# A hybrid decoder trunk on one core: block order, a delayed sum and an earlier last norm in the second layer's down stage

## The chip, the cores and the metric

The kernel runs on one core of a Trainium2 chip. The metric is device time in microseconds (us), from the start to the end of one execution; a kernel's time is the median of its runs. The core has five engines with a queue of instructions each: TensorE (PE, matmuls, with its weight loads listed as PEld), VectorE (DVE), ScalarE (ACT), GpSimd (POOL), and SyncE (SP), which here only issues transfers. Each queue is worked off in order: an instruction that waits holds up everything behind it on its engine. Transfers run beside the engines.

## The reference

Two layers, each a token mixer and a feed-forward part (SwiGLU), each with an RMSNorm that is shifted and scaled by a conditioning vector in front, and a gated residual sum behind. The sequence has 1024 tokens of 1024 channels, the feed-forward part 2816 hidden channels. The stack ends with one more RMSNorm. Cut to what matters here:

```
def swiglu_ffn(h, w_gate, w_up, w_down):
    return (jax.nn.silu(h @ w_gate) * (h @ w_up)) @ w_down

for i in range(DEPTH):                      # DEPTH = 2
    ...
    y = swiglu_ffn(h, ffn_w_gate[i], ffn_w_up[i], ffn_w_down[i])
    x = x + (1.0 + g_f)[:, None, :] * y
return rms_norm(x, final_g)
```

All in float32. The change is in how the last `@ w_down` (i = 1), the last sum into x, and the last `rms_norm` are ordered.

## The kernel before

**Layout.** x is held with channels on the 128 partitions: eight tiles of 128 channels for each of two chunks of 512 tokens, chunk A (first) and chunk B. A float32 operand is split into a high part (a cast on ScalarE) and a low part (the difference, on VectorE); a product is then three matmuls: high by high, high by low, low by high (`products`). Every matmul goes through line 148, every recorded operation of VectorE, ScalarE and GpSimd through line 126 and the transfers of SP through lines 158 and 1449; so the profile's lines say little, and the tile names tell the operations apart: `dn` is a bank of the down product, `w` a weight's parts, `raw` and `s` weights as loaded or summed, `op` an operand as loaded, `hi` and `lo` its parts, `t` and `acc` squares and their sums, `var` the mean of squares and `rstd` the reciprocal root spread over the partitions, `ny` its copy.

**Seven products.** The second layer's down product is done with seven block products (Strassen's way) instead of eight. The weight is split in four blocks by even and odd hidden tiles and by the two halves of the output channels, the operand by even and odd hidden tiles and by the two chunks. Class `Seven` runs a list of steps: each block product (p2, p1, p5, p6, p7, p4, p3) is a loop over groups q = 0 to 5 of hidden tiles. Eleven pairs of tiles make five full groups of two (24 matmuls) and one short one, q = 5, with one (12 matmuls). p2's groups 0 to 3 are done earlier (`one_half`); p3's groups in `LAST` = (2, 3, 4) are left to `ending`.

Two sets of four PSUM banks, x and y, collect the products. p2 uses y; p1 starts x; p5 starts y; p6, p7 and p4 go on adding to what is in x; p3 starts y. With the last group of each block product, as soon as a bank has its last matmul, `update` on VectorE adds gate times the bank to the x tile of a chunk and half:

```
last = q == qs[-1] and j == len(ops) - 1
products(bs[d], wt, 4 * j + d, g, fresh and q == qs[0] and j == 0, last, more=True)
if last:
    for ch, half in ends:
        update(ch, 4 * half + d, bs[d], gate_f, self.l)
```

Within a group the banks are worked in two pairs, (0, 1) and then (2, 3), each over the group's one or two operand tiles. The next block product on the same banks cannot write a bank before its update has read it.

**Weights and operands of a group.** `weights_of` loads the weight block on SP; for `s1` (p5) and `s4` (p3) a second load on POOL's queue adds another block to it in flight, and can start only when the first has landed. A block of sums (`st["sum", q]`, tile `s`) is held over the stage: p1 loads a11 into it, p5 takes its own sum off it, p6 uses it as its weight, p7 adds it to its load, p3 adds a12 to it and uses it. `halves` makes the parts of the weight; in p5 it also issues the subtraction from the held block, right behind the weight's low part and ahead of the operand's parts. `operand` loads the operand (written to memory by the joint stage before: the last store, for group 5, is made at the end of that stage). `Seven.load` runs LOADED = 4 groups ahead, `Seven.split` SPLIT = 2 groups ahead. Chunk B's x comes back from memory in four transfers, m = 0 to 3, one behind each of p1's groups q = 0 to 3 (`x_in`, the dictionary given to `seven.run`).

**What sets the order.** TensorE's order is the order of the code. On the other engines a scheduler places the instructions by a simulated timeline and by priority; `tc.add_manual_dep(later, earlier, edge)` fixes the order of two. Background work is written as generators (`Task`) that `pace` steps between groups of matmuls, by model clocks of the engines. A generator may yield a name; the task then rests until the model clock of TensorE has passed the later of VectorE's and ScalarE's clocks by a delay from these tables (the second for a task in the background, as here):

```
DELAY = {"stats": 2.75, "spread": 3.0, "soon": 0.5, "settled": 3.0, "later": 5.0, "root": 3.4}
DELAY_BEHIND = {"stats": 8, "spread": 4, "soon": 0.5, "settled": 3.0, "later": 8}
```

**The last norm.** `final(A)` is such a task. It squares and sums chunk A's tiles (the second half once p4 is through), then calls `mean_rsqrt`: rest by `when`, matmuls for the mean, eight short VectorE instructions for the reciprocal root, rest, matmuls that spread the root, a copy. Then it multiplies the eight tiles, five on GpSimd, three on VectorE, and stores them. Chunk B's last norm is in `ending`: p3's last groups and B's first output half, in two halves of 256 tokens, four banks each, with the updates, squares and sums on the way, and a norm for each half.

Of the kernel before, what the change touches and what calls it, by code (L numbers as in the profile page):

```python
# [14 lines left out]
MUL, ADD, SUB = ALU.mult, ALU.add, ALU.subtract  # L15
# [45 lines left out]
NQ = -(-NP // 2)  # L61
LAST = (2, 3, 4)
# [69 lines left out]
def trunk(ctx, tc, xT, c, vec, ada, adan, w1f, w1, wdg, w2, wgu, wdn, wds, wpl, out):  # L132
# [3 lines left out]
    V_ = Engine(nc.vector, "V", clock, PRICES["V"], lambda i: order(i))  # L136
# [391 lines left out]
        V_.scalar_tensor_tensor(y, t, 1.5 * 0.375, y, op0=ADD, op1=MUL)  # L528
        yield

    def mean_rsqrt(acc, n, keep=False, when="stats", loose=False, early=False):

        count = n // P
        parts = acc if isinstance(acc, list) else [acc]
        yield when
        b = bank("var")
        for i in range(count):  # L540
            for a in parts:
                matmul(b[:, i : i + 1], a[:, i * P : (i + 1) * P], ones[:, 0:1], start=a is parts[0], stop=a is parts[-1])
        v, t = b[:, :count], b[:, 16 : 16 + count]
        cols = tmp.tile([P, 16], F32, tag="col1", name=nm("col"), bufs=1)
        col, q = cols[:, :count], cols[:, 8 : 8 + count]
        for _ in rsqrt(v, col, t, q, "T" not in st or "taps_done" in st):
            if loose:
                yield
        V_.spent += 0.2
        clock["V"] += 0.2  # L550
        done = V_.last.ins.name
        for ins in [] if loose else recent + (beside if early else []) + [lows[id(wt)][0] for wt in st.get("loaded", [])[1:] if id(wt) in lows]:
            tc.add_manual_dep(ins, done, edge, reason="behind the root")
        recent.clear()
        yield "spread" if loose else "root"
        r = spare_bank("rstd") if "taps_done" in st else bank("rstd")
        for i in range(count):
            matmul(r[:, i * P : (i + 1) * P], col[:, i : i + 1].broadcast_to([P, P]), ident, start=True, stop=True)
        r = r[:, :n]
        if not keep:  # L560
            return r
        held = temp(n, "ny", 2)
        S_.copy(held, r)
        return held
# [94 lines left out]
    def unit(emit, *weights):  # L659
        units.append((weights, emit))  # L660
# [765 lines left out]
    def weights_of(l, kind, q, placed=True):  # L1426

        n = duo_width(q) * 512
        src = lambda b: wds[q, b][:, :n]
        got = {}  # L1430

        def behind_products(d):
            if placed and last_mm[0] is not None:
                tc.add_manual_dep(d.ins, last_mm[0], edge, reason="behind the products")

        def plus(r, what):
            behind_products(nc.gpsimd.dma_start(r, what, accum_op=ADD))
            clock["G"] = max(clock["G"], clock["PE"]) + 0.9

        def load():  # L1440
            if kind == "a11":
                st["sum", q] = block("h1", "s", F32).rearrange("p a b -> p (a b)")[:, :n]
            if kind in ("a11", "s2", "s4"):
                r = st["sum", q]
            else:
                r = (raw_tile() if placed else raws.tile([P, D], F32, tag="raw", name=nm("raw")))[:, :n]
            first = {"a11": 0, "a12": 1, "a22": 3, "s1": 2, "s3": 3}.get(kind)
            if first is not None:
                behind_products(nc.sync.dma_start(r, src(first)))
            if kind in ("s1", "s4"):  # L1450
                plus(r, src(3 if kind == "s1" else 1))
            got["raw"] = r

        def halves():
            r = got["raw"]
            if kind == "s3":
                V_.tensor_tensor(r, r, st["sum", q], op=ADD)
            wt = wts.tile([P, 2, D], F32R, tag="w", name=nm("w"))
            S_.copy(wt[:, 0, :n], r)
            V_.tensor_tensor(wt[:, 1, :n], r, wt[:, 0, :n].bitcast(F32), op=SUB)  # L1460
            if kind == "s1":
                V_.tensor_tensor(st["sum", q], st["sum", q], r, op=SUB)
            return wt

        return load, halves
# [23 lines left out]
    class Seven:  # L1489
# [13 lines left out]
        def split(self, upto):  # L1503
            while self.splits < min(upto, len(self.parts)):
                self.ready[self.splits] = [part[1]() for part in self.parts[self.splits]]
                self.splits += 1

        def begin(self):
# [132 lines left out]
    def final(ch):  # L1641
        acc = temp(ch.n, "acc", 2)
        for k in range(KT):
# [6 lines left out]
            elif k:  # L1650
                V_.tensor_tensor(acc, acc, sq, op=ADD)
            yield
        steps = mean_rsqrt(acc, ch.n, True, loose=True)
        yield next(steps)
        for k in range(KT):
            S_.activation(x[ch.i][k], x[ch.i][k], AF.Copy, scale=V("final_g", k))
# [273 lines left out]
    def pool_end(ch):  # L1930
# [14 lines left out]
    heads(1, HEADS[1], lambda: None)  # L1945
    unit(lambda take: calm.__setitem__(0, True))
    pool_end(B)
    every = list(range(NQ))
    short = [q for q in every if q not in LAST]
    seven = Seven(1, [  # L1950
        ("p2", "a12", "b21", "y", True, [(A, 0)], [4, 5]),
        ("p1", "a11", "b11", "x", True, [(A, 0)], every),
        ("p5", "s1", "t1", "y", True, [(B, 1), (B, 0)], every),
        ("p6", "s2", "t2", "x", False, [(B, 0)], every),
# [8 lines left out]
    def final_begins():  # L1963
# [2 lines left out]

    seven.run({
        **{("p1", m): lambda m=m: unit(lambda take: x_in(B, m)) for m in range(KT // 2)},
        ("p7", NQ - 1): final_begins,
        ("p4", NQ - 1): lambda: unit(lambda take: st.__setitem__("a_done", True)),  # L1970
    }, last_part)
    run_units(W_BUFS, early)

# [60 lines left out]
```

## Time and profile before

| what | value |
|---|---|
| median of 3 runs | 1707.15 us (1706.41 to 1709.43) |
| the profiled execution | 1708.65 us |
| its span, first to last instruction | 1706.9 us |
| TensorE busy | 1671.0 us, 98% of the span |
| VectorE, ScalarE, GpSimd busy | 77%, 47%, 28% |
| granted TensorE clock, mean | 0.996 of full speed |
| seven products | from about 1492.6 us of the span |
| end of the last product | about 1689.1 us |

The profile is one execution. A row of the timeline gives the start (us from the span's start), the length, the engine, the line, the operation with out<-in and shapes, the count of merged instructions, and in brackets how long the engine was idle before and what ended that. The row of a tile gives the shortest, median and longest length in ns. A row of stretches gives start:end, the length, busy time and count for each engine, then the granted clock, the mean busy share of the 16 transfer engines, and GB/s. A row of the chain gives start, length and what the end of the kernel waited for. Matmuls overlap, so a row of several matmuls is longer than their spacing.

### The profile page before, as it was taken

Reading aid. Unit: us, or ns where it says so; the run is one execution under the profiler, and the core shown is the slowest. Engines: PE = TensorE matmul, PEld = TensorE weight load, DVE = VectorE, ACT = ScalarE, POOL = GpSimd, SP = SyncE. Lnnn points to the kernel's source line nnn. Section 1 sums busy time; section 2 is a strip of 40 time slices with the busy share of each in tenths; the row PEclk is TensorE's granted clock in tenths of the full one; section 3 lists DMA queues with packets and bytes.
Section 4 is the critical chain, followed back from the end, with each engine's and each line's share of the span. In section 5 each row is a group of like instructions: output and inputs, shape, how many; then the busy total and the mean of one; then the engine's idle time right before and its main releaser. Section 6 shows DMA issues by size and latency. Waiting matters only on the chain.

```text
span 1706.9 us, 21328 instructions
## 1 busy us (share of the span) xinstructions
PE 1671.0 (98%) x7614; PEld 1361.9 (80%) x7614; DVE 1318.9 (77%) x1872; ACT 799.5 (47%) x1085; POOL 483.1 (28%) x566
## 2 busy tenths in 40 slices
PE   7999999999999999999999999999999999999996
PEld 5777777778887888888888888888888888887776
DVE  8889899899659887878665987858777767657575
ACT  3669686866546333333213446637222222334353
POOL 3587767796001111211110311101111111010103
PEclk9999999999999999999999999999999999999998
DMA  8858987827776788986877757866777777486822
GB/s 303 286 168 228 237 229 196 220 96 225 225 238 152 253 272 279 294 249 229 342 256 264 250 173 206 241 237 190 189 209 234 217 229 217 169 294 191 241 93 99
DMA packets 115821, 380.71 MB, mean 223 GB/s; under 512 B 12225, under 2 KB 14401, under 8 KB 115714
## 3 DMA queue, kind: packets, MB, share of 16 engines
q1 hardware_dynamic: 77888, 247.46, 41.0%
q0 software_dynamic: 36736, 130.83, 31.2%
q8 instruction: 60, 0.98, 0.2%
q10 hardware_dynamic: 1090, 1.05, 0.2%
q14 instruction: 47, 0.39, 0.1%
HBM read 311.92 MB, written 63.18 MB: 220 GB/s over the span
## 4 chain that ended last, share of the span: by engine, by line
PE 86%; DVE 6%; DMA 3%; ACT 1%; issue 1%; POOL 1%; SPq 0%; DVEq 0%; ACTq 0%
PE a L148 23%; PE dn L148 21%; PE e L148 13%; PE p L148 12%; PE y L148 6%; PE g L148 3%; PE first L148 3%; PE tap L148 2%; DMA raw<-in_wds_dram 2%; POOL pa L126 1%; PE ada L148 1%; DVE t L126 1%; DMA adaw<-in_adan_dram 1%; DMA op<-kinds 1%; DVE x L126 1%
## 5 line engine op out<-in xcount | busy, mean ns | idle before, releaser
L126 ACT CAST w<-raw 128x1024 fp32r<-128x1024 f32 (+1 forms) x249 | 258.9, 1041 | 365.2 <-PE dn L148 99.7
L148 PE MATMUL dn<-g,w 128*128 128x512 f32 x1152 | 265.2, 391 | 1.7 <-DVE g L126 1.0
L126 DVE TENSOR_TENSOR w<-raw,w 128x1024 fp32r<-128x1024 f32 x177 | 217.7, 1233 | 51.2 <-ACT w L126 50.9
L148 PEld LDWEIGHTS dn<-g,w 128*128 128x128 f32 x1152 | 215.7, 188 | 47.6 <-DVE g L126 1.3
L148 PE MATMUL a<-n,w 128*128 128x512 f32 x1056 | 247.7, 390 | 1.1 <-DVE n L126 0.7
L148 PE MATMUL p<-h,w 128*128 128x512 f32 x1056 | 244.2, 391 | 0.9 <-DVE h L126 0.7
L126 POOL TENSOR_TENSOR pa<-pa,pr 128x512 f32<-128x512 f32 x160 | 228.4, 1512 | 23.0 <-ACT pr L126 16.6
L148 PEld LDWEIGHTS a<-n,w 128*128 128x128 f32 x1056 | 197.9, 188 | 44.0 <-DVE n L126 2.2
L148 PEld LDWEIGHTS p<-h,w 128*128 128x128 f32 x1056 | 197.3, 188 | 43.8 <-DVE h L126 1.5
L148 PE MATMUL dn<-hi,w 128*128 128x512 f32 (+1 forms) x600 | 174.3, 373 | 4.3 <-DVE x L126 2.4
L126 DVE SCALAR_TENSOR_TENSOR ca<-u,vecs,ca 128x512 f32<-128x512 f32 x245 | 169.7, 745 | 0.5
L126 DVE SCALAR_TENSOR_TENSOR x<-dn,gains,x 128x512 f32<-128x512 f32 (+1 forms) x144 | 100.9, 730 | 44.7 <-PE dn L148 44.6
L148 PEld LDWEIGHTS dn<-hi,w 128*128 128x128 f32 x600 | 109.8, 188 | 25.6 <-DVE x L126 3.2
L148 PE MATMUL a<-t,w 128*128 128x512 f32 x528 | 123.6, 390 | 0.7 <-DVE w L126 0.7
L148 PE MATMUL e<-b,w 128*128 128x512 f32 x528 | 123.4, 390 | 0.6 <-DVE r L126 0.6
L148 PE MATMUL e<-t,w 128*128 128x512 f32 x528 | 123.3, 389 | 0.0
L126 ACT ACTIVATE pr<-u,vecs 128x512 f32<-128x512 f32 x160 | 108.2, 716 | 26.0 <-POOL pa L126 18.2
L148 PEld LDWEIGHTS a<-t,w 128*128 128x128 f32 x528 | 99.0, 188 | 21.6 <-DVE w L126 1.1
L148 PEld LDWEIGHTS e<-b,w 128*128 128x128 f32 x528 | 99.1, 188 | 21.5 <-DVE r L126 1.0
L1108 POOL DMA_DIRECT2D raw<-in_wgu_dram x41 | 36.2, 884 | 282.5 <-DVE r L126 78.3
L148 PEld LDWEIGHTS e<-t,w 128*128 128x128 f32 x528 | 99.1, 188 | 20.5
L148 PE MATMUL dn<-lo,w 128*128 128x512 f32 (+1 forms) x300 | 111.7, 372 | 0.0
(181 smaller groups left out, 2380.2 us busy)
## 6 DMA issues: line engine op xcount, KB each, us to landing
raw<-in_wgu_dram SPq DMA_DIRECT2D x132, 512.0 KB, 4.8
adaw<-in_ada_dram POOLq DMA_DIRECT2D x48, 512.0 KB, 7.3
raw<-in_wdn_dram SPq DMA_DIRECT2D x44, 512.0 KB, 8.1
raw<-in_wgu_dram POOLq DMA_DIRECT2D x41, 512.0 KB, 7.4
raw<-in_w_dram SPq DMA_DIRECT2D x36, 512.0 KB, 6.2
gd<-g POOLq DMA_DIRECT2D x36, 512.0 KB, 8.1
g<-gd SPq DMA_DIRECT2D x36, 512.0 KB, 6.0
kinds<-k POOLq DMA_DIRECT2D x33, 512.0 KB, 7.3
```

The costliest lines, as they stand in the source:

```text
L126: self.last = self.order(getattr(self.eng, name)(out, *args, **kw))
L148: last_mm[0] = nc.tensor.matmul(out, lhsT, rhs, start=start, stop=stop, skip_group_check=more).ins.name
L1108: d = order(nc.gpsimd.dma_start(w[i], wgu[l, fp, src], accum_op=ADD))
```

## The change

Three things. First, the groups' order in the block products: p1, p5, p6, p7 and p4 run 0, 1, 2, 5, 3, 4 in place of 0 to 5, p2 runs 5, 4 in place of 4, 5, and p3's part in `Seven` runs 0, 5, 1 in place of 0, 1, 5. So each block product ends with a full group; the hooks that hung on the last group of p7 and p4 follow it. The four returns of x stay with groups 0 to 3 of p1. Second, in p5 the subtraction from the held block is issued after the operand's parts, and an order edge puts it behind the operand's low part on VectorE. Third, in `final` the rest ahead of the mean's matmuls becomes "settled" (3.0 in place of 8 for "stats"), and the rest ahead of the spread becomes "soon" (0.5 in place of 4 for "spread").

```
-    def mean_rsqrt(acc, n, keep=False, when="stats", loose=False, early=False):
+    def mean_rsqrt(acc, n, keep=False, when="stats", loose=False, early=False, then=None):
...
-        yield "spread" if loose else "root"
+        yield then or ("spread" if loose else "root")
...
             if kind == "s1":
-                V_.tensor_tensor(st["sum", q], st["sum", q], r, op=SUB)
+                st["then_sum"] = lambda: V_.tensor_tensor(st["sum", q], st["sum", q], r, op=SUB)
...
                 self.ready[self.splits] = [part[1]() for part in self.parts[self.splits]]
+                low = V_.last.ins.name
+                if "then_sum" in st:
+                    tc.add_manual_dep(st.pop("then_sum")().ins, low, edge, reason="behind the low parts")
                 self.splits += 1
...
-        steps = mean_rsqrt(acc, ch.n, True, loose=True)
+        steps = mean_rsqrt(acc, ch.n, True, "settled", loose=True, then="soon")
...
-    every = list(range(NQ))
-    short = [q for q in every if q not in LAST]
+    every = [0, 1, 2, 5, 3, 4]
+    short = [0, 5, 1]
     seven = Seven(1, [
-        ("p2", "a12", "b21", "y", True, [(A, 0)], [4, 5]),
+        ("p2", "a12", "b21", "y", True, [(A, 0)], [5, 4]),
         ("p1", "a11", "b11", "x", True, [(A, 0)], every),
         ("p5", "s1", "t1", "y", True, [(B, 1), (B, 0)], every),
         ("p6", "s2", "t2", "x", False, [(B, 0)], every),
         ("p7", "s3", "t3", "x", False, [(B, 1)], every),
         ("p4", "a22", "t4", "x", False, [(A, 1)], every),
         ("p3", "s4", "b22", "y", True, [(B, 0)], short),
...
-        ("p7", NQ - 1): final_begins,
-        ("p4", NQ - 1): lambda: unit(lambda take: st.__setitem__("a_done", True)),
+        ("p7", every[-1]): final_begins,
+        ("p4", every[-1]): lambda: unit(lambda take: st.__setitem__("a_done", True)),
```

## The prediction

> **What bounds the kernel now.** I read the page first, then the stretches of the second layer's down stage, then TensorE's own timeline there, and last the queues that its waits point to.
>
> ```profile
> PE 1671.0 (98%) x7614; PEld 1361.9 (80%) x7614; DVE 1318.9 (77%) x1872; ACT 799.5 (47%) x1085; POOL 483.1 (28%) x566
> ```
>
> TensorE is busy for 98% of the span, so only its idle stretches and the tail can give time. The stretches (times from the span's start; busy time and count for each engine; then granted clock, DMA share, GB/s):
>
> ```profile
> core 0: us, PE busy (x) PEld busy (x) DVE busy (x) ACT busy (x) POOL busy (x), PEclk, DMA share, GB/s
> 1492.60:1543.64 51.04, 49.56 (x219) 40.74 (x217) 30.02 (x34) 15.67 (x18) 5.97 (x8) 1.00 0.92 292
> 1594.76:1626.49 31.73, 30.46 (x132) 24.63 (x132) 17.62 (x20) 12.86 (x17) 3.54 (x4) 1.00 0.83 237
> 1669.40:1689.10 19.70, 19.68 (x166) 19.44 (x164) 11.20 (x30) 9.78 (x21) 1.46 (x1) 1.00 0.00 1
> 1689.10:1706.90 17.80, 4.77 (x20) 4.42 (x20) 7.89 (x24) 1.67 (x4) 11.68 (x13) 0.59 0.66 236
> 1506.84:1530.71 23.87, 23.87 (x107) 19.75 (x106) 7.24 (x7) 4.57 (x6) 1.79 (x3) 1.00 0.94 308
> ```
>
> The stage starts near 1492.6, its last products end near 1689.1, and 17.8 us of tail follow in which TensorE works 4.8 us. The transfers are nearly full before 1543 and empty from 1669 to 1689. TensorE's timeline (start, length, instruction, idle before it and what ended that) shows all its idle time:
>
> ```profile
> 1543.64 0.74 PE L148 MATMUL dn<-hi,w 128*128 128x512 f32 x2 [1.48 <-DVE w L126]
> ...
> 1594.76 0.50 PE L148 MATMUL dn<-hi,w 128*128 128x512 f32 x1 [1.59 <-DVE x L126]
> ...
> 1624.79 0.47 PE L148 MATMUL dn<-hi,w 128*128 128x512 f32 x1 [0.50 <-ACT w L126]
> ...
> 1626.49 0.50 PE L148 MATMUL dn<-hi,w 128*128 128x512 f32 x1 [0.77 <-DVE x L126]
> ...
> 1692.70 1.23 PE L148 MATMUL rstd<-ident,col 128*128 128x128 f32 x4 [3.62 <-DVE col L126]
> ```
>
> That is 4.34 us of idle in the products, and 3.62 us in front of the ending's first reciprocal root. Together 7.96 us: the most that the change can take from TensorE's waits.
>
> **The unit of time.** From the chain of waits:
>
> ```profile
> 1492.75 24.27 PE dn L148 x107
> ```
>
> 0.227 us for a matmul: a full group (24 matmuls) takes 5.44 us, the short group (12) 2.72 us.
>
> **Part 1, the short group in the middle: the ends of blocks.** Products p1, p6, p7, p4 accumulate in the same four banks, and after each the bank's sum is added to x. The next product may not write bank 0 before VectorE has read it. With the short group last, bank 0 is done 0.68 us into that group, bank 1 at 1.36, and they are wanted at 2.72 and 3.40: 2.04 us for each. With a full group last they are done at 2.04 and 2.72 and wanted at 5.44 and 6.12: 3.40 us. The end of p6 on VectorE:
>
> ```profile
> 1591.03 0.75 DVE L126 SCALAR_TENSOR_TENSOR x<-dn,gains,x 128x512 f32<-128x512 f32 x1
> 1591.69 1.22 DVE L126 TENSOR_TENSOR lo<-op,hi 128x1024 fp32r<-128x1024 f32 x1
> 1592.82 1.22 DVE L126 TENSOR_TENSOR raw<-raw,s 128x1024 f32<-128x1024 f32 x1
> 1593.96 0.75 DVE L126 SCALAR_TENSOR_TENSOR x<-dn,gains,x 128x512 f32<-128x512 f32 x1
> ```
>
> TensorE sat idle for 1.59 us up to 1594.76, so bank 1 was wanted near 1593.1 (a little before, by the pipeline) and done 2.04 us ahead of that, near 1591.1; its read ended at 1594.71, 3.6 us behind. A window of 3.40 us leaves 0.2 us of that as idle if lo and raw stay between, nothing if the planner now lets the read pass one of them. Bounds 0 and 1.59; I take **1.4**. The end of p7:
>
> ```profile
> 1621.36 1.23 DVE L126 TENSOR_TENSOR w<-raw,w 128x1024 fp32r<-128x1024 f32 x1 [0.29 <-ACT w L126]
> 1622.50 1.48 DVE L126 TENSOR_TENSOR acc<-acc,t 128x512 f32<-128x512 f32 x2
> 1623.90 0.74 DVE L126 SCALAR_TENSOR_TENSOR x<-dn,gains,x 128x512 f32<-128x512 f32 x1
> ...
> 1625.70 0.74 DVE L126 SCALAR_TENSOR_TENSOR x<-dn,gains,x 128x512 f32<-128x512 f32 x1
> ```
>
> Here the reads stood behind a weight split that waited for a late load, and behind two sums of squares. The loads come by buffers and by TensorE's steps, not by this order, so a full last group alone doesn't help; it helps only if the two sums (1.48 us) now go behind the reads, which become ready 1.36 us sooner against the loads. Bounds 0 and 1.27 (0.50 + 0.77); I take half, **0.63**.
>
> **Part 1 again: the loads of p5.** The third group of p5 has late weights (SP's and POOL's queues, then VectorE):
>
> ```profile
> 1514.05 0.60 SPq L158 DMA_DIRECT2D x<-xd  x1
> 1514.69 0.43 SPq L1449 DMA_DIRECT2D raw<-in_wds_dram  x1
> ...
> 1530.71 0.86 POOL L1437 DMA_DIRECT2D raw<-in_wds_dram  x1 [7.80 <-DMA op<-kinds]
> ...
> 1528.36 1.22 DVE L126 TENSOR_TENSOR w<-raw,w 128x1024 fp32r<-128x1024 f32 x1
> ...
> 1540.09 1.23 DVE L126 TENSOR_TENSOR s<-s,raw 128x1024 f32<-128x1024 f32 x1 [3.11 <-DMA raw<-in_wds_dram]
> ...
> 1542.37 1.22 DVE L126 TENSOR_TENSOR w<-raw,w 128x1024 fp32r<-128x1024 f32 x1
> ```
>
> Its first load is issued at 1514.69, the adding load on POOL can start only at 1530.71, its data is there at 1540.1, the low part ends at 1543.6. The last return of x (x<-xd, 512 KB, 1.7 us at 308 GB/s) stands in front of it on SP. In the code this return hangs on p1's group 3, which the new order puts behind group 5; so it falls behind this load. That is worth up to 1.70, more than the 1.48 of idle, but the same queue's operand loads shift too, and p5's groups 3 and 4 are wanted 2.72 us sooner. By bytes they are ready in time: three full groups and a half weigh less than four. Bounds -1.5 (the wait doubles) and 1.48; I take **1.0**.
>
> **Part 2, the sum behind the low parts.** It is six VectorE instructions of 1.23 us, moved, none added. The row at 1540.09 shows a sum 1.14 us ahead of the low part that TensorE waits for. But the new edge ties it to the low part of the group's operand, and for this group that ran long before:
>
> ```profile
> 1533.79 1.22 DVE L126 TENSOR_TENSOR lo<-op,hi 128x1024 fp32r<-128x1024 f32 x1
> ```
>
> So the order stands as it is, and the part is worth **0** (bounds 0 and 1.14, and the latter is inside the 1.48 above).
>
> **Part 3, the first chunk's last norm.** Its delays fall by 5.0 ("stats" 8 to "settled" 3) and 3.5 ("spread" 4 to "soon" 0.5) of the planner's microseconds; it issues nothing new: 8 small matmul records for the mean, 8 for the spread, one copy, 5 multiplies on POOL, 3 on VectorE, 4 stores of 512 KB on SP.
>
> ```profile
> 1673.78 0.95 PE L148 MATMUL var<-ones,acc 128*128 128x1 f32 x8
> 1685.88 1.05 PE L148 MATMUL rstd<-ident,col 128*128 128x128 f32 x8
> ...
> 1663.51 0.68 DVE L126 SCALAR_TENSOR_TENSOR acc<-t,acc 128x512 f32<-128x512 f32 x1
> ...
> 1687.59 0.69 DVE L126 TENSOR_TENSOR x<-x,ny 128x512 f32<-128x512 f32 x1
> 1689.37 2.35 DVE L126 TENSOR_TENSOR x<-x,ny 128x512 f32<-128x512 f32 x2
> ...
> 1691.70 0.47 DVE L126 SCALAR_TENSOR_TENSOR x<-dn,gains,x 128x256 f32<-128x256 f32 x1
> ...
> L126 POOL TENSOR_TENSOR x<-x,ny x13: 722/726/1782, 1687.6 to 1700.7; 128x256 f32<-128x256 f32 x8, 128x512 f32<-128x512 f32 x5
> L126 DVE TENSOR_TENSOR x<-x,ny x3: 677/691/1745, 1687.6 to 1690.0; 128x512 f32<-128x512 f32 x3
> ```
>
> The sum of squares is ready at 1664.2, its mean matmul stands at 1673.78 in TensorE's order and the spread at 1685.88, ahead of the last product. So the three multiplies fall exactly where the last update should run: that update, wanted at 1689.1, runs at 1691.70, and the second chunk's root waits behind the same multiplies; TensorE idles 3.62 us. With 5.0 the mean comes near 1668, 4 us behind its inputs; with 8.5 the spread comes near 1677. Five multiplies of up to 1.78 on POOL end by about 1687, beside products, and the four stores fall in the stretch with empty queues. Then the last update ends near 1689.6, the first root stands ready at 1689.1, and the tail moves up by nearly all of the 3.62. Against it: at "soon" TensorE may wait for the spread's input. Bounds 0 and 3.62; I take **3.0**, half a microsecond off for such a wait. The stores' earlier issue I count at nothing: the second chunk's stores still come last. Nor do I count the granted clock, 0.59 in the tail, which may stay higher if the idle goes.
>
> **The sum.** 1.4 + 0.63 + 1.0 + 0 + 3.0 = 6.0 us. The profiled execution took 1708.65 us with a span of 1706.9, so 1702.6 and 1700.9; the median of the three runs is 1707.15, 1.5 us below that execution, and from it follows **1701.1**.
>
> **Rivals.**
>
> *Only the tail.* VectorE's queue waits for loads at both block ends and at p5, and the stalls move along with them. For it: the p7 rows, and a DMA share of 0.83 to 0.94. Against it: the p6 rows name no load. 3.0 saved at the tail alone: **1704.1**.
>
> *The tail gives it back.* The multiplies now run beside the ending's sums, and POOL's hold up VectorE's: 1.745 against 0.677 us in the rows above, 1.07 a time. The last of the first half's four sums and its mean on TensorE:
>
> ```profile
> 1680.15 0.42 DVE L126 TENSOR_TENSOR acc<-acc,t 128x256 f32<-128x256 f32 x1 [0.48 <-ACT t L126]
> ...
> 1683.30 0.50 PE L148 MATMUL var<-ones,acc 128*128 128x1 f32 x4
> ```
>
> 2.7 us to spare, four sums at 1.07 each are 4.3: 1.6 us paid on TensorE, and as much once more for the short root instructions behind. Against it: VectorE works 11.2 of 19.7 us there. With nothing of the tail's gain left: 3.0 saved at the products, **1704.1**. [...]
>
> *Slower: SP's queue is held sooner.* SP waits 11.0 us up to 1506.84 for one thing, the short operand of p1, whose store is the last of the joint stage:
>
> ```profile
> 1506.84 1.65 SPq L158 DMA_DIRECT2D op<-kinds  x3
> ...
> SPq L158 <- DMA kinds<-k: 11.0, 1, 11.0
> ```
>
> The change puts that operand two places earlier. If it keeps that place on SP, five and a half loads of 512 KB that are through by then go behind it: 2.88 MB at 308 GB/s, 9.4 us for p5's loads. The low part of p5's first group ended at 1529.6, against a start of that group near 1530.7 and a third matmul near 1531.1: 1.5 us to spare. All p5 comes 9.4 us late, its own 1.0 us of gain falls away, and 5.0 us are gained elsewhere: **1711.5**. It makes the kernel slower from a delay of 6.5 us on (1.5 + 5.0). Against it: the planner put that operand behind other loads before, and may again.
>
> *It does nothing that can be measured*, each gain met by a wait of its size: **1707.1**.
>
> **How the numbers follow.** Forecast 0.48; only the tail 0.18; the tail gives it back 0.15; SP's queue 0.12; nothing 0.07. A measurement of this kernel tells about 0.2% (3.4 us) from no change: faster means under 1703.7, slower over 1710.6. Faster: nearly all of the forecast (0.46) and some 0.4 of the two with 1704.1 (0.14), 0.60. Slower: nearly all of the rival on SP's queue, 0.11. Within: the rest, 0.29. The forecast's own range is 1699 (all 7.96 us) to 1703; the other cases on the same side carry the upper end to 1706.5, and half a microsecond for a higher clock in the tail and earlier stores, neither of which the rows price, carries the lower to 1698.5.
>
> **What would show it.** Right: no idle over 0.3 us at the start of p7; the first chunk's spread on TensorE before 1680, POOL's five wide multiplies before 1689; the last update within 1 us of the last product. Wrong: SP's wait for the kinds store ahead of p1's weight loads; a wait of over 1 us before the first chunk's spread; p5's third group waiting 1.5 us or more.

## The result and the profile after

The changed kernel took 1697.58 us (median; 1697.23 to 1702.04) against 1708.29 us for the kernel before in the same session: a ratio of 0.9943 with a 95% interval of 0.9923 to 0.9964, that is -9.7 us (-13.2 to -6.2). The ratio is that of the means of the runs (1698.6 and 1708.3 us); the medians differ by 10.7 us. Measured once more among the experiments it gave 0.9950 (0.9938 to 0.9962), -8.5 us. It is faster, as forecast, and by more than the 6.0 us of the forecast: both medians (1697.58 and 1698.44) lie just under the range's lower end of 1698.5. One of the twelve executions of the kernel "loads early" below took 2092.53 us at a granted clock of 0.75 and is left out of its numbers.

The profiled execution took 1702.04 us. The page's first line and the two stretches of the stage, products and tail (columns as in the prediction: busy time and count for PE, PEld, DVE, ACT, POOL, then granted clock, DMA share, GB/s):

```profile
span 1700.3 us, 21323 instructions
...
1494.60:1687.84 193.24, 191.77 (x923) 161.26 (x922) 130.93 (x161) 86.15 (x113) 20.17 (x20) 1.00 0.62 192
1687.84:1700.30 12.46, 3.03 (x20) 2.59 (x19) 4.63 (x17) 1.57 (x4) 5.54 (x8) 0.62 0.50 169
```

Before, the products took 196.5 us (1492.6 to 1689.1) and the tail 17.8. So the products are 3.25 us shorter and the tail 5.36: 8.6 us for the stage. The stage began 2.0 us later in this execution than in that of before, in work that the change does not touch; over all profiles of this case its start wandered from 1491.8 to 1497.0. Lengths within the stage are therefore a better measure of one profile than its span.

All of TensorE's idle time in the stage, from its timeline (start, length, instruction, idle before it and what ended that):

```profile
1593.91 0.47 PE L148 MATMUL dn<-hi,w 128*128 128x512 f32 x1 [1.06 <-DVE x L126]
...
1597.34 0.50 PE L148 MATMUL dn<-hi,w 128*128 128x512 f32 x1 [0.41 <-DVE x L126]
...
1689.06 0.38 PE L148 MATMUL var<-ones,t 128*128 128x1 f32 x2 [0.44 <-ACT t L126]
...
1691.85 1.19 PE L148 MATMUL rstd<-ident,col 128*128 128x128 f32 x4 [1.74 <-DVE col L126]
```

Gone are p5's 1.48, p4's 0.50 + 0.77 and the tail's 3.62. Still there is the start of p7: 1.59 before, 1.06 + 0.41 now. The reason stands on VectorE's queue (start, length, operation):

```profile
1586.13 1.23 DVE L126 TENSOR_TENSOR raw<-raw,s 128x1024 f32<-128x1024 f32 x1 [4.77 <-DMA raw<-in_wds_dram]
...
1593.02 1.41 DVE L126 SCALAR_TENSOR_TENSOR x<-dn,gains,x 128x512 f32<-128x512 f32 x2
...
1595.39 1.23 DVE L126 TENSOR_TENSOR raw<-raw,s 128x1024 f32<-128x1024 f32 x1 [0.97 <-DMA raw<-in_wds_dram]
```

VectorE waits 4.77 us for one of p7's weights, then works off 6.9 us of splits that piled up behind it, and only then reads p6's banks (the x rows).

The tail's turn is seen on TensorE, VectorE and GpSimd:

```profile
1665.48 0.95 PE L148 MATMUL var<-ones,acc 128*128 128x1 f32 x8
...
1673.41 1.05 PE L148 MATMUL rstd<-ident,col 128*128 128x128 f32 x8
...
1687.68 0.60 PE L148 MATMUL rstd<-ident,col 128*128 128x128 f32 x4
...
1675.12 4.09 DVE L126 TENSOR_TENSOR x<-x,ny 128x512 f32<-128x512 f32 x3
...
1680.10 0.56 DVE L126 TENSOR_TENSOR acc<-acc,t 128x256 f32<-128x256 f32 x1 [0.48 <-ACT t L126]
...
1687.88 0.48 DVE L126 SCALAR_TENSOR_TENSOR x<-dn,gains,x 128x256 f32<-128x256 f32 x1 [1.67 <-PE dn L148]
...
1675.17 8.07 POOL L126 TENSOR_TENSOR x<-x,ny 128x512 f32<-128x512 f32 x5 [69.26 <-ACT ny L126]
```

The first chunk's mean stands at 1665.5 (1673.8 before) and its spread at 1673.4 (1685.9 before). GpSimd's multiplies are over at 1683.2. The ending's first root (four rstd matmuls at 1687.68) follows the last product with no idle time, and the last update runs at 1687.88, 0.04 us behind the last product, where it was 2.6 us behind.

### The profile page after: what moved, and what is told of

Its sections match the earlier page's. It is cut to its first block, busy times and chain, and to the rows that moved or that the text cites. A ratio compares the mean times of both kernels' runs of the same rounds, so it can differ in the third digit from the quotient of the medians.

```text
span 1700.3 us, 21323 instructions
## 1 busy us (share of the span) xinstructions
PE 1670.4 (98%) x7614; PEld 1361.6 (80%) x7614; DVE 1319.5 (78%) x1872; ACT 800.3 (47%) x1085; POOL 481.9 (28%) x566
## 3 DMA queue, kind: packets, MB, share of 16 engines
q10 hardware_dynamic: 1090, 1.05, 0.2%
## 4 chain that ended last, share of the span: by engine, by line
PE 88%; DVE 5%; DMA 3%; issue 1%; POOL 1%; ACT 1%; SPq 0%; DVEq 0%; ACTq 0%
PE a L148 24%; PE dn L148 23%; PE e L148 13%; PE p L148 12%; PE y L148 6%; PE g L148 3%; PE first L148 3%; PE tap L148 2%; DMA raw<-in_wds_dram 1%; POOL pa L126 1%; PE ada L148 1%; DMA adaw<-in_adan_dram 1%; DVE t L126 1%; PE rstd L148 1%; PE var L148 1%
## 5 line engine op out<-in xcount | busy, mean ns | idle before, releaser
L126 DVE TENSOR_TENSOR w<-raw,w 128x1024 fp32r<-128x1024 f32 (+1 forms) x177 | 217.9, 1234 | 50.4 <-ACT w L126 49.9
```

The costliest lines, as they stand in the source:

```text
L126: self.last = self.order(getattr(self.eng, name)(out, *args, **kw))
```

## The experiments

Times are against the kernel before on the same chip; products, idle and tail come from each kernel's profile (first of the seven products to the last, and from there to the end).

| kernel | ratio (95%) | products | idle in them | tail |
|---|---|---|---|---|
| before | | 196.5 | 4.34 | 17.8 |
| after | 0.9943 (0.9923 to 0.9964) | 193.2 | 1.47 | 12.5 |
| after, again | 0.9950 (0.9938 to 0.9962) | 191.9 | 0.35 | 12.1 |
| groups' order alone | 0.9984 (0.9975 to 0.9993) | 192.7 | 0.91 | 17.8 |
| last norm alone | 0.9965 (0.9953 to 0.9978) | 194.3 | 1.94 | 12.2 |
| moved sum alone | 1.0011 (1.0002 to 1.0020) | 196.2 | 2.83 | 17.4 |
| order and norm, no moved sum | 0.9958 (0.9945 to 0.9972) | 192.2 | 0.35 | 11.9 |
| spread rests 4 again | 0.9946 (0.9931 to 0.9961) | 193.2 | 1.44 | 14.5 |
| mean rests 8 again | 0.9957 (0.9941 to 0.9974) | 191.9 | 0.35 | 15.2 |
| return of x early | one execution, 1698.34 us | 192.9 | 1.07 | 11.9 |
| return of x late | one execution, 1708.97 us | 197.6 | 3.11 | 17.8 |
| reads first | 0.9978 (0.9969 to 0.9986) | 197.5 | 3.41 | 12.4 |
| loads early | 0.9988 (0.9978 to 0.9998) | 201.4 | 7.09 | 11.9 |
| both | 0.9977 (0.9967 to 0.9986) | 196.9 | 2.82 | 12.4 |

### The three parts one by one

**The groups' order alone** (the lists `every` and `short`, p2's order and the two hooks, as in the change):

```
+    every = [0, 1, 2, 5, 3, 4]
+    short = [0, 5, 1]
```

> The groups' new order alone, in the kernel before; the sum and the last norm stay as they were. Theory (three gains in three places): the order is worth what TensorE's idle in the products lost in the changed kernel, 4.34 us before less 1.47 us after, so about 2.9 us; the wait at p5's third group (1.48 us) and the two at the start of p4 (1.27 us) are gone, the one at the start of p7 stays near 1.5 us, and the 3.62 us in front of the ending's root stay too. About 2.9 us faster than the kernel before. Rival (the gain is all in the tail, TensorE's waits in the products move with other things): no difference, within 1 us.

Measured: 1704.39 us, -2.7 us (-4.3 to -1.2). TensorE's idle rows:

```profile
1590.91 0.47 PE L148 MATMUL dn<-hi,w 128*128 128x512 f32 x1 [0.56 <-ACT hi L126]
...
1594.28 0.50 PE L148 MATMUL dn<-hi,w 128*128 128x512 f32 x1 [0.35 <-DVE x L126]
...
1688.45 1.17 PE L148 MATMUL rstd<-ident,col 128*128 128x128 f32 x4 [3.62 <-DVE col L126]
```

p5 and p4 run without a wait, p7's start keeps 0.91 us, and the tail is that of before, with its 3.62. So with the order alone p5 and p4 run clear. For p5 this one profile does not show that the order did it: p5 waits in one of the three profiles with the old order and the return in its place (before), and not in the other two (the norm alone and the moved sum alone, below).

**The last norm alone:**

```
-        steps = mean_rsqrt(acc, ch.n, True, loose=True)
+        steps = mean_rsqrt(acc, ch.n, True, "settled", loose=True, then="soon")
```

> The first chunk's last norm alone, in the kernel before; the groups' order and the sum stay. Theory (three gains in three places): the tail behind the last product falls from 17.8 us to about 12.5 us, so 5.3 us faster than the kernel before, and the four waits in the products stay at 4.3 us together. Rival (the norm can move forward only because the new order ends p4 with a full group, whose updates come sooner): under 3 us faster, with a wait of TensorE in front of the first chunk's mean or spread.

Measured: 1701.05 us, -6.0 us (-8.0 to -3.8): two thirds of the change's gain. Its products keep waits at p7 and p4 (1.17 and 0.77 us) but show none at p5, so 1.94 us in place of the 4.3 expected; its tail is 12.2 us.

**The moved sum alone** (the edge behind the low part, in the old order):

```
-                V_.tensor_tensor(st["sum", q], st["sum", q], r, op=SUB)
+                st["then_sum"] = lambda: V_.tensor_tensor(st["sum", q], st["sum", q], r, op=SUB)
```

> The sum behind the low parts alone, in the kernel before; order and norm stay. Theory (the part is empty): the scheduler had placed each sum behind its operand's low part already but for one group, the short last one of p5, where nothing waits; no difference, within 0.5 us, and the wait at p5's third group stays near 1.5 us. Rival (the sum ahead of the low part is what made TensorE wait there): 1.1 us faster and the wait under 0.4 us.

Measured: 1707.66 us, +1.9 us (0.3 to 3.4), no gain. The order of VectorE's instructions differs from before only in the short group of p5, where the sum now runs last (`s` behind `lo`):

```profile
1550.41 0.69 DVE L126 TENSOR_TENSOR lo<-op,hi 128x512 fp32r<-128x512 f32 x1
1551.01 0.68 DVE L126 TENSOR_TENSOR s<-s,raw 128x512 f32<-128x512 f32 x1
```

p5 had no wait in this profile. But its third group's low part, wanted by TensorE 49.4 us into the stage, was ready only 0.45 us ahead of that; in the profile of the norm alone, where p5's order is that of before, it was ready 0.16 us behind, and in that of before 1.59 us behind. So the missing wait looks like the scatter of a load's landing; the third group's rows stand in the old order in all three. What the profile does show to cost something is the clock behind the two waits at p4 (TensorE's windows of 2 us):

```profile
1622.00:1624.00 2.00, 0.93 (x3) 0.48 (x3) 2.00 (x4) 2.00 (x4) 0.00 (x0) 1.00 0.42 170
1624.00:1626.00 2.00, 1.98 (x5) 1.61 (x6) 2.00 (x3) 2.00 (x5) 0.00 (x0) 0.59 0.58 159
1626.00:1628.00 2.00, 2.00 (x6) 1.51 (x5) 2.00 (x3) 2.00 (x6) 0.00 (x0) 0.56 0.66 235
1628.00:1630.00 2.00, 2.00 (x10) 1.69 (x9) 2.00 (x4) 2.00 (x5) 0.00 (x0) 1.00 0.45 136
```

Waits of 0.94 and 0.77 us, and the granted clock falls to 0.59 and 0.56 for 4 us: 5 and 6 matmuls in 2 us in place of 10. The same place before, with waits of 0.50 and 0.77, kept 1.00 from 1618 to 1640. Without their idle time these products took 193.4 us, those of before 192.2: 1.3 us more, which is my estimate of the clock's price. Whether the +1.9 us of the median comes from that is not settled.

**Order and norm without the moved sum** (the change with the subtraction left where it was):

> The order and the norm without the moved sum: the changed kernel less its second part. Theory (the part is empty, the two others add up): the instructions stand in the same order on every engine as in the changed kernel, so the same time: 8 to 10 us faster than the kernel before. Rival (the moved sum carries a part): 1 us or more slower than the changed kernel's 1697.6 us, with a wait at p5's third group.

Measured: 1699.71 us, -7.2 us (-9.4 to -4.8). Its instructions stand in the same order as those of the changed kernel, on every engine and in every row: with the short group in the middle the edge binds nothing. So this run, the change's own and its repetition are three measurements of one order of instructions: 0.9943, 0.9950 and 0.9958. The parts add up: -2.7 and -6.0 make -8.7.

### Is it the return of x that p5 waited for?

The forecast put p5's gain on the last return of x, which the new order drops behind the load of p5's third group on SP. If so, moving the return alone must move the wait. (The scheduler answers each of the two edits with another order of a few instructions in p5 on VectorE, so not only the return moves.)

**Return early**: the changed kernel with the fourth return one group sooner, so that it is again ahead of that load; **return late**: the kernel before with the return one group later, so that it is behind it.

```
-        **{("p1", m): lambda m=m: unit(lambda take: x_in(B, m)) for m in range(KT // 2)},
+        **{("p1", every[m]): lambda m=m: unit(lambda take: x_in(B, m)) for m in range(KT // 2)},       # early
+        **{("p1", (0, 1, 2, 4)[m]): lambda m=m: unit(lambda take: x_in(B, m)) for m in range(KT // 2)},  # late
```

> The changed kernel with the fourth return of x hung on p1's group 5, the fourth in the new order, so that on SP it stands ahead of the load of p5's third group again. Theory (the return's 512 KB in front of that load made p5 late): the low part of that group's weight, 1.6 to 2.3 us ahead of its use in three profiles with the new order, is 1.7 us later: between 0.6 us ahead and 0.1 us late. Rival (the readiness comes from the group order itself, with the short group's smaller loads): still 1.6 us or more ahead.

> The kernel before with the fourth return of x hung on p1's group 4 in place of 3, nothing else: in the old order the return goes behind the load of p5's third group. Theory (the return): that group's low part, 1.6 us late, 0.15 late and 0.45 us ahead of its use in three profiles with the old order, comes 1.7 us sooner, 1 us or more ahead. Rival (the group order): no sooner than in those three.

Measured, TensorE's idle rows in the products, the early return first:

```profile
1542.66 0.74 PE L148 MATMUL dn<-hi,w 128*128 128x512 f32 x2 [1.07 <-DVE w L126]
```

and the late one:

```profile
1591.06 0.47 PE L148 MATMUL dn<-hi,w 128*128 128x512 f32 x1 [1.21 <-DVE x L126]
...
1593.90 0.79 PE L148 MATMUL dn<-hi,w 128*128 128x512 f32 x1 [1.90 <-DVE x L126]
```

The return's place moves p5's loads, in either order of the groups. The first load of p5's third group took 14.5 to 15.4 us from issue to landing in the four profiles with the return in front of it (before, norm alone, moved sum alone, return early) and 11.6 to 13.8 us in the seven with the return behind it (return late and the six of the new order that keep the return in its place). With the return late the low part comes 4.5 us ahead of its use; in the three profiles of the old order it came from 1.6 us behind to 0.45 ahead. That is more than the 1.7 us of the theory, and why is not shown.

With the return early a wait is back (1.07), but VectorE's order made it:

```profile
1538.48 1.22 DVE L126 TENSOR_TENSOR s<-s,raw 128x1024 f32<-128x1024 f32 x1 [0.66 <-DMA raw<-in_wds_dram]
1540.78 0.69 DVE L126 TENSOR_TENSOR s<-s,raw 128x512 f32<-128x512 f32 x1 [1.07 <-DMA raw<-in_wds_dram]
1541.39 1.82 DVE L126 TENSOR_TENSOR w<-raw,w 128x1024 fp32r<-128x1024 f32 x2
```

The third group's weight was there for the first of these rows, and ScalarE's copy of it was done at 1539.6. But the short group's sum (the second row) now stands ahead of the third group's low part (the third) and waits 1.07 us for its own load. Without it the low part would have been ready some 0.7 us ahead of its use (an estimate from these rows), as the theory had it. So the return early brings the late load back and not, by itself, the wait.

But the time does not follow: 1698.34 us in one execution of the early one, as fast as the changed kernel, and 1708.97 us for the late one, no faster than before. The early one has no wait at p7's start, the late one 3.1 us. In the late one VectorE's sum ahead of p6's reads started 97.3 us into the stage, as in the kernel before, and TensorE came to p7 some 1.8 us sooner. Behind its second wait matmuls of one shape started 0.43 us apart until 1599.6 (three in 1.28 us), and 0.23 us apart from 1600.4 on: without their idle time its products took 194.5 us, against 192.2 before. That p7 loses what p5 gains is no rule, though: the norm alone and the moved sum alone did not wait at p5 either, the same sum started 95.3 and 95.0 us into the stage there, and p7's start waited 1.17 and 1.12 us, less than the 1.59 of before.

### How much room does the first chunk's norm need?

The change's two delays undone one at a time: the spread's rest back to 4 ("spread"), and the mean's back to 8 ("stats").

```
-        steps = mean_rsqrt(acc, ch.n, True, "settled", loose=True, then="soon")
+        steps = mean_rsqrt(acc, ch.n, True, "settled", loose=True)               # spread rests 4
+        steps = mean_rsqrt(acc, ch.n, True, loose=True, then="soon")             # mean rests 8
```

> The changed kernel with the rest ahead of the spread back at 4 (spread), the rest ahead of the mean still 3 (settled). In TensorE's order the first chunk's spread then stands 72 matmuls of the ending ahead of its end, against 108 in the changed kernel and 18 in the kernel before. Theory (the gain is the room between the spread and the last update, about 5 us of copy and multiplies): 72 matmuls are 8.6 us, enough; the wait in front of the ending's first root stays at nothing and the time is that of the changed kernel within 1 us. Rival (each delay brings its share of the tail's 5.3 us, 3.5 of 8.5 parts for this one): about 2.2 us slower than the changed kernel.

> The changed kernel with the rest ahead of the mean back at 8 (stats), the rest ahead of the spread still 0.5 (soon). The spread then stands 36 matmuls, 4.3 us, ahead of the end. Theory (room): the spread, its copy and three multiplies take some 5.5 us and end 1 us or a little more behind the last product; a wait of 1 to 1.5 us stays in front of the first root, and the kernel is 1.5 to 2.5 us slower than the changed one. Rival (each delay brings its share, 5 of 8.5 parts for this one): about 3.1 us slower than the changed kernel with a wait near 2 us.

Measured, in the order of TensorE's instructions: how many of the ending's 432 product matmuls stand behind the first chunk's spread, and how long TensorE then waits for the ending's first root.

| kernel | matmuls behind the spread | wait for the first root | tail |
|---|---|---|---|
| groups' order alone (8, then 4) | 18 | 3.62 | 17.8 |
| mean rests 8 (8, then 0.5) | 36 | 1.48 | 15.2 |
| spread rests 4 (3.0, then 4) | 72 | 0.60 | 14.5 |
| after (3.0, then 0.5) | 108 | 0 | 12.5 |

```profile
1685.72 0.71 PE L148 MATMUL rstd<-ident,col 128*128 128x128 f32 x4 [0.60 <-DVE col L126]
```

```profile
1690.41 0.71 PE L148 MATMUL rstd<-ident,col 128*128 128x128 f32 x4 [1.48 <-DVE col L126]
```

The first row is the spread at 4, the second the mean at 8. Neither delay does it alone: the wait shrinks with the room behind the spread and is gone only with both. The theory had expected no wait at 72 matmuls; 0.60 us was measured. The waits are nearer the theory, but the tails, 2.0 to 2.4 and 2.7 to 3.1 us longer than in the two profiles of the change, are what the rival had put on each delay (2.2 and 3.1). The whole times, 9.2 and 7.4 us under the kernel before, cannot be told from that of the change by their intervals, so between theory and rival this stays open.

### What holds p7's start?

One wait is left in the products, 0.35 to 1.47 us at p7's start in profiles of the changed kernel. Two ways to take it away, and both together, beside the changed kernel once more.

**Reads first**: VectorE's work on the weights of the next three groups is put behind its read of the second bank at the ends of p6 and p7. **Loads early**: p7's weights are loaded two groups sooner, each ahead of the operands.

```
+    def gated_order(ins):                                        # reads first
+        if gate[0] is not None:
+            tc.add_manual_dep(ins.ins, gate[0], edge, reason="behind the reads")
+        return order(ins)
...
+            while self.weights < min(upto + (2 if self.kinds[min(self.weights, len(self.kinds) - 1)] == "s3" else 0), len(self.parts)):   # loads early
+                self.parts[self.weights][0][0]()
+                self.weights += 1
```

> The changed kernel once more, beside the three kernels that it is compared with. Both theories of p7's start expect what its first profile showed: VectorE waits some 4 to 5 us for p7's next weight load ahead of its reads of p6's banks, TensorE idles 0.2 to 1.5 us at the start of p7, nothing at the start of p4, and the tail takes 12 us. Time 7 to 10 us under the kernel before.

> VectorE's work on the next three groups' weights is held behind its reads of the first two banks at the ends of p6 and p7; loads are issued as before. Theory one (the idle at p7's start is the order on VectorE: the reads stand behind a weight that is still on its way): no idle over 0.2 us at the start of p7, and 0.2 to 1.5 us less than the changed kernel beside it, as much as that one idles there. Theory two (the late load itself is the limit): the reads come in time, but p7's second group then waits for its weights, 1 to 2 us some 5 us into p7, and the time stays within 0.5 us of the changed kernel.

> p7's weight loads are issued two groups earlier on SP, and each ahead of its group's operand; VectorE's order is the planner's. Both theories: VectorE's wait of 4 to 5 us for that load goes, and with it the idle at p7's start, so 0.2 to 1.5 us less than the changed kernel. A third (the loads' bytes are the limit, the transfers being 0.83 to 0.94 busy): what is loaded sooner pushes back an operand or a later load by 1.7 us each, and a wait of 1 to 3 us appears at the end of p6 or in p4; the time then stays or grows by 1 us.

> Both edits together. Theory one and two: no idle over 0.2 us in the seven products beside p5's third group; 0.2 to 1.5 us less than the changed kernel, no more than the better of the two alone. Third theory: as for the loads alone.

Measured: 1703.63, 1705.21 and 1703.68 us, against 1698.44 us for the changed kernel: all three 5 to 7 us worse, where the theories had expected 0.2 to 1.5 us of gain, or at worst 1 us of loss. TensorE's idle rows, reads first (the edit moves the line numbers by 7):

```profile
1624.12 0.50 PE L155 MATMUL dn<-hi,w 128*128 128x512 f32 x1 [1.62 <-DVE x L126]
...
1628.25 0.50 PE L155 MATMUL dn<-hi,w 128*128 128x512 f32 x1 [1.79 <-DVE x L126]
```

p7's start is clear, as theory one says, and p4's start, clear in the changed kernel, waits 3.4 us. VectorE at that place:

```profile
1619.50 0.74 DVE L126 SCALAR_TENSOR_TENSOR x<-dn,gains,x 128x512 f32<-128x512 f32 x1
1622.71 0.69 DVE L126 TENSOR_TENSOR acc<-acc,t 128x512 f32<-128x512 f32 x1 [2.46 <-ACT t L126]
1623.32 0.74 DVE L126 SCALAR_TENSOR_TENSOR x<-dn,gains,x 128x512 f32<-128x512 f32 x1
1623.98 1.22 DVE L126 TENSOR_TENSOR w<-raw,w 128x1024 fp32r<-128x1024 f32 x1
...
1627.45 0.74 DVE L126 SCALAR_TENSOR_TENSOR x<-dn,gains,x 128x512 f32<-128x512 f32 x1
```

The second wait is the edit's own: the splits that it holds back run right behind the second read (1623.98 and on), ahead of the third and fourth. The first is a sum that stands between the reads and waits 2.46 us for a square. The chain of waits follows that back to loads (start, length, what):

```profile
1596.02 0.61 DVE lo L126
...
1596.65 0.52 SPq L165
...
1597.22 14.90 DMA raw<-in_wds_dram
...
1615.70 0.52 SPq L165
...
1616.27 4.63 DMA raw<-in_wds_dram
...
1621.00 0.62 ACT w L126
1621.62 0.53 ACT acc L126
1622.16 0.53 ACT t L126
```

On SP an operand load waits for the low part (`lo`) that frees its buffer, and the next weight load is behind it; so a split that VectorE does later issues loads later. Counted from the start of the seven products, the load at 1597.22 (p4's first weight) went out 0.8 us later than in the second profile of the changed kernel and took 14.9 us to land against 13.8 there, the operand load at 1615.70 2.0 us later. The weight behind that one holds ScalarE's copy (`w`), and behind the copy stand the squares (`acc`, `t`). The granted clock fell after these waits as well, to 0.71 and 0.50 in the two stretches of 2 us from 1628 on: without their idle time these products take 194.1 us, against 191.6 in the second profile of the changed kernel.

Loads early, on VectorE and on TensorE:

```profile
1594.38 1.23 DVE L126 TENSOR_TENSOR raw<-raw,s 128x1024 f32<-128x1024 f32 x1 [9.70 <-DMA raw<-in_wds_dram]
...
1598.15 0.77 PE L148 MATMUL dn<-hi,w 128*128 128x512 f32 x1 [7.09 <-DVE x L126]
```

The wait that was to go doubled, and it is for another load: in the changed kernel it is that of p7's third group, here that of its last, whose sum now stands ahead of p6's reads on VectorE. That load went out at 1580.18 and was there 14.1 us later; the median of the weight loads from 1559 to 1601 there is 6.5, and the same load took 9.9 in the second profile of the changed kernel. GpSimd's rows, loads early first, then the second profile of the changed kernel:

```profile
1578.36 2.65 POOL L1437 DMA_DIRECT2D s<-in_wds_dram  x3 [9.00 <-ACT hi L126]
1582.94 0.87 POOL L1437 DMA_DIRECT2D s<-in_wds_dram  x1 [1.93 <-DVE w L126]
```

```profile
1588.80 2.65 POOL L1437 DMA_DIRECT2D s<-in_wds_dram  x3 [14.39 <-DVE raw L126]
1595.16 0.87 POOL L1437 DMA_DIRECT2D s<-in_wds_dram  x1 [3.71 <-DVE x L126]
```

p3's adding loads may start when p7 has used the held sum. With p7's weights summed sooner, four of them start 10 to 12 us sooner and are on their way together with that load. So loads do meet, as the third theory says, but at another place, and the order on VectorE makes it cost 7.1 us and not 1 to 3. That these four loads are what made it 14.1 us was not tried. In the kernel with both edits the reads go first again, and the waits are those at p4's start (0.74 + 1.80 + 0.28).

So the wait at p7's start is what it looked like, reads queued behind a weight that is late. The profiles of the new order say the same: VectorE's sum behind that load started 89.96, 90.15, 90.24, 91.02, 91.53 and 91.65 us into the stage in six of them, and TensorE then waited 0.17, 0.35, 0.35, 0.91, 1.47 and 1.44 us at p7's start; with the return early it started at 88.75 and there was no wait. But VectorE's order also paced the loads of SP (0.8 and 2.0 us later with the reads first) and of GpSimd (10 to 12 us sooner with the loads early), and both ways of clearing it cost more than it is worth. Nothing tried here beats the changed kernel.

## Why the prediction was right, and where not

**The ends of blocks, p6 to p7 (1.4 forecast).** This is the step that failed. "A window of 3.40 us leaves 0.2 us" took the read as late as it was before, behind a low part and a sum. "The p6 rows name no load" held only for the rows shown: the row right ahead of them, in the profile before, waits for one.

```profile
1589.89 1.23 DVE L126 TENSOR_TENSOR raw<-raw,s 128x1024 f32<-128x1024 f32 x1 [1.30 <-DMA raw<-in_wds_dram]
```

In the new order the scheduler put the reads behind more work, not less: the sum that waits for p7's third weight, five splits and one more sum, 6.9 us from 1586.13 to 1593.02, all of it starting when that weight lands. This eats the longer window. The six profiles of the change and its variants that have the new order and the return in its place had 0.17 to 1.47 us there (mean 0.78), the three old ones with the return in its place 1.12 to 1.59 (mean 1.29). The gain is nearer 0.5 than 1.4 us. The rival "only the tail" had said that VectorE waits for loads at both block ends and that the stalls move along with them; for this term it was right about the loads. Why that weight lands up to 1.7 us later in one profile of the new order than in another stays open.

**p7 to p4 (0.63).** Undersized: all of 1.27 went, since six of seven profiles with the new order show no wait at p4's start and the seventh 0.18 us. The condition that the step had set was met. Before, two sums stood ahead of the first read and a low part of 1.21 us between the first two reads; in the changed kernel

```profile
1622.89 0.74 DVE L126 SCALAR_TENSOR_TENSOR x<-dn,gains,x 128x512 f32<-128x512 f32 x1
1623.56 0.68 DVE L126 TENSOR_TENSOR acc<-acc,t 128x512 f32<-128x512 f32 x1
1624.15 0.74 DVE L126 SCALAR_TENSOR_TENSOR x<-dn,gains,x 128x512 f32<-128x512 f32 x1
```

no sum stands ahead and one between. The reads still stand behind a late split, as the step had it, and end 1.05 and 0.47 us ahead of TensorE's first matmuls on these banks (1624.68 and 1625.36). Two sums ahead of them took 1.40 us before (1622.50 to 1623.90), which would have used that up (an estimate). So the mechanism held, and the half was too little.

**p5's third group (1.0).** That the return of x makes this load late is shown by its landing times (14.5 to 15.4 us with the return in front, 11.6 to 13.8 behind it), and with the return late the wait was gone; with it early the load was late again, but the wait seen there had another cause. In the changed kernel the wait of 1.48 went whole, and no other group of p5 took it over. But it was there in one of three profiles of the old order, so its mean is 0.5 us and not 1.48. Terms one and three together were put at 2.4 us; the idle time at p5 and p7 fell by 1.6 in the first profile and 2.7 in the second, counted from the profile before, and by 0.3 and 1.4 counted from the mean of the three old ones. The order alone, with p4's term, was measured at 2.7 us against 3.0 forecast. That these two are so near is luck: p7's term was too large by 0.9 us, p4's too small by 0.6, and p5's depends on the profile it is read from.

**The moved sum (0).** Right: with the new order it changes no row.

**The tail (3.0).** The mechanism is the one forecast, the size was short, and this term alone is most of what the sum of 6.0 us lacks: 5.4 us in the first profile, 5.7 in the second, and 5.6 with the norm alone. The idle time fell from 5.64 us (3.62 + 2.02) to 2.18 (0.44 + 1.74), that is by 3.46, and no wait ahead of the spread came in to take the half microsecond that was held back. The rest is what the forecast named and did not count, the granted clock: TensorE's 20 instructions in the tail were busy for 4.77 us and now for 3.03. The first root takes 0.60 us in place of 1.23: the granted clock is 1.00 where it runs now (1687 to 1689) and was 0.50 from 1693 on before.

**The rivals.** *The tail gives it back* is refuted, though longer rows beside GpSimd are there: of VectorE's three multiplies beside GpSimd's, two took 1.78 us each and one 0.69 (before, one 1.75 and two 0.68 and 0.69). But the price on the sums was 0.14 us each (0.56 while GpSimd's multiplies ran, up to 1683.2, against 0.42 behind them), not the 1.07 taken from the wide multiplies, which held for two of the three of these, and no wait of TensorE came of it. *SP's queue is held sooner* did not happen: SP's wait for that store ended 11.1 us into the stage, against 14.2 before, and p5's first load went out 14.5 us into it, against 16.6. *Only the tail* had 1704.1 us; the order's own gain of 2.7 us speaks against it. *It does nothing that can be measured* is refuted by the ratio.

**The signs.** Spread before 1680: 1673.4. The five wide multiplies before 1689: over at 1683.2. Last update within 1 us of the last product: 0.04 us to its start. No idle over 0.3 us at p7's start: wrong, 1.06.

## What to carry to other kernels

Clearing a wait that loads pace may move it to the next place where TensorE meets the same queue, as it did with the return late and did not in two other kernels; so ask of every removed wait where those loads are met next. A wait that one profile shows may be absent from the next one of the same order, so read several before it is priced. An engine off the critical path may be the one that frees buffers: before its instructions are moved, look at which queue waits for them and what that queue then issues. A chunk's last work, moved ahead of the kernel's tail, paid twice here: by the wait that went (3.46 us of idle time), and by short matmuls that then ran at a higher clock (1.00 where the first root runs, 0.59 to 0.50 before; 1.74 us).

## What the hardware showed that was not expected

The granted clock fell to near half behind short waits. In the kernel with the moved sum 1.71 us of idle within 2.6 us were followed by 4 us at 0.56 to 0.59; before, 1.27 us at the same place were followed by 1.00 throughout. After 3.41 us of waits in 5.8 us (reads first) it was 0.50 to 0.71 for 4 us. The longest single wait among these was 1.79 us. What makes the clock fall is not shown.

Nor was the clock behind a given wait the same each time: the second root of the tail, 1.74 and 1.73 us after the previous matmul, took 1.19 us for its four matmuls in the first profile of the changed kernel (granted clock 0.50 from 1692 to 1694, 0.62 over the tail) and 0.80 in the second (1688.62; 0.68 over the tail), with the same instructions ahead of it.

```profile
1688.62 0.80 PE L148 MATMUL rstd<-ident,col 128*128 128x128 f32 x4 [1.73 <-DVE col L126]
```
